# A fused decoder layer in float32: pads between the tiles of split weights, and a smaller tile of ones

## The chip, the cores and the metric

The kernel runs on one core of a Trainium2 chip. Five engines work side by side: TensorE (PE in the profile, its weight loads PEld), VectorE (DVE), ScalarE (ACT), GpSimd (POOL) and SyncE (SP), which here issues all DMA transfers. Tiles lie in the on-chip buffer, 128 partitions of some 224 KB each; every tile has one start address that is the same in all partitions, and where this text speaks of addresses it means that one, in bytes. Products are summed in PSUM. The metric is the time of one execution on the device in microseconds: the median of three runs. Matmuls are counted start to start where their pace is meant; the duration that the profile gives for one is longer, since they are pipelined.

## What is computed

One layer of a decoder trunk on a sequence of 1,024 positions and 1,024 features, all in float32:

```python
h = rmsnorm(x, mix_norm)
q, k, v, su, sv, g_a, g_b = split(h @ w_in)          # 512, 128, 128, 512, 512, 1024, 1024 columns
y_att = sliding_window_attention(q, k, v, ...)       # 8 query heads, 2 key heads, window 128
y_sgu = gelu(su) * (tril(w_s) @ rmsnorm(gelu(sv)) + b_s)
merged = sigmoid(g_a) * (y_att @ w_oa) + sigmoid(g_b) * (y_sgu @ w_ob)
x = x + merged @ w_out
z = conv3(rmsnorm(x) @ w_up)                          # 1024 -> 2 * 2816, causal width 3 per channel
x = x + (silu(z_gate) * z_val) @ w_down
```

## The kernel before

**Split products.** A float32 product is made of three matmuls in a format (R in the code) that keeps fewer bits: each operand is split into a rounded part h and a rest l, and h·h, h·l and l·h are summed. ACT copies the tile into h (`copy_hi`, line 75), POOL or DVE subtracts (for weights `wsplit`, line 91, and `Left.split`, line 975). So weights exist as a raw tile, an h tile and an l tile, 128 partitions by 1,024 numbers (4,096 bytes) each.

**Stages.** (1) k, v and q projections while x arrives (matmuls of 256 columns; `pkv`, `pq`), beside them the row sums of x squared, in `rstd_b`, a buffer of one row of 1,024 numbers that later holds the norm's factor. (2) Attention in blocks of 128 queries, with the u projection (`pu`) as filler. (3) The v projection of the spatial gate (`pvs`), whose second half of weights, `wvB`, lies in the pool zr on the right side of the buffer, and the mixing (`pm`). (4) The gates, from 221 us: each pair of column blocks is one step of a 2 by 2 Strassen-like scheme (`Blocks`, line 1000, its matmuls at line 1017) with seven products of twelve matmuls of 512 columns; the moving operands are B11, B21, B22 and the sums T1 to T4, of which T3 now lies in zr; the stationary ones are the split weights p (A11, A12), q (S1, A22), s3 (S3) and r (S2, S4; its halves lie in a tile AX). (5) Eight branch products twice and eight output tiles, `po` and `px` (lines 79 to 81), by a list of jobs. (6) 22 pairs of the up projection, with the same scheme as the gates (`fast_pair`, line 1489), T3 now in another pool (ex), s3 in a pool wx; the convolution and the gating run on DVE and ACT beside them. (7) The down projection (line 1661), again seven products.

**Order.** PE's order is written by hand from stage 2 on (`manual_schedule`), and the other engines' order too from there; in stage 1 a scheduler sets the order of the engines other than PE. SP's queue carries all DMAs in program order.

**Allocation.** A pool lays its tiles out in the order in which the program first asks for them, rounded up to 32 bytes. From the bottom stand: `base` (constants, `ones`, `rstd_b`, small columns, `msk`), `big` (eight tiles of 16,384 bytes: x, weights of q, later all large row tiles), `wst` (the split weights), then pools that are opened and closed by stage; from the top stand the right side's pools. In `wst` come three raw tiles, then, by tag and with two buffers each, h, h, l, l; a request with a tag takes the buffer that is free next. Tiles of 32 bytes named pad_l, pad_r and pad_z stand in three stage pools. Modulo 512, all of `big` and `wst` start at 0 (xf at 7,680, the raw tiles from 138,752, h at 151,040 and 155,136, l at 159,232 and 163,328); zr's tile starts at 212,928, which is 448 modulo 512.

**At the start.** POOL fills `ones` (128 by 128) and `mh05`; PE does seven warm-up products of `ones` with `ones` (line 209) while the first x is on its way; `affine_select` (line 150) makes the mask from `ones`; `ssq` (line 306) and `ssq_cols` (line 1343) use two columns of it.

Of the kernel before, what the change touches and what calls it, by code (L numbers as in the profile page):

```python
# [10 lines left out]
F = mybir.dt.float32  # L11
R = mybir.dt.float32r
# [22 lines left out]
def build(tc, a):  # L35
    nc = tc.nc
    ctx = ExitStack()
    with ctx, tc.manual_schedule(engines={mybir.EngineType.PE}):
        body(ctx, tc, nc, a)


def body(ctx, tc, nc, a):
    L, H = slice(0, 512), slice(512, 1024)
    base = ctx.enter_context(tc.tile_pool(name="base", bufs=1))
    big = ctx.enter_context(tc.tile_pool(name="big", bufs=1))
    wst = ctx.enter_context(tc.tile_pool(name="wst", bufs=2))
# [3 lines left out]
    def nm(s):  # L50
        uid[0] += 1
        return f"{s}_{uid[0]}"

    def Y(s, dt=R, shape=None):
        return big.tile(shape or [128, 4, 1024], dt, tag="Y", name=nm(s), bufs=7)
# [10 lines left out]
    def PH(s):  # L66
        if psum.get("H") is None:
            return PS(s)[:, 0:512]
        return psum["H"].tile([128, 512], F, tag="H", name=nm(s))

    def raw(s):
        return wst.tile([128, 8, 128], F, tag="raw", name=nm(s), bufs=3)

    def copy_hi(dst, src, scale=1.0):
        return nc.scalar.activation(dst, src, AF.Copy, scale=scale)  # L75

# [11 lines left out]
    def wtile(src, s, nk=8):  # L88
        return wsplit(wload(src, s, nk), s, nk)

    def wsplit(r, s, nk=8):

        h = wst.tile([128, 8, 128], R, tag="wh", name=nm(s + "h"))
        l = wst.tile([128, 8, 128], R, tag="wl", name=nm(s + "l"))
        copy_hi(h[:, :nk, :], r[:, :nk, :])
        nc.gpsimd.tensor_tensor(l[:, :nk, :], r[:, :nk, :], h[:, :nk, :].bitcast(F), op=ALU.subtract)  # L96
        return h, l
# [2 lines left out]
    cp = base.tile([128, 194], F, name="cp")  # L100
    sink_b = base.tile([128, 8], F, name="sink_b")
    ident = base.tile([128, 128], F, name="ident")
    ones = base.tile([128, 128], F, name="ones")
    rstd_b = base.tile([128, 1024], F, name="rstd_b")
    mh05 = base.tile([128, 8], F, name="mh05")
    rstd = base.tile([128, 8], F, name="rstd")
    nc.gpsimd.memset(ones, 1.0)
    nc.gpsimd.memset(mh05, -0.5)
    g2 = cp[:, 0:8]
# [3 lines left out]
    def rsqrt_cols(dst, ss, n, width):  # L113

        nc.vector.tensor_scalar(dst, ss, 1.0 / width, EPS, op0=ALU.mult, op1=ALU.add)
        return nc.gpsimd.tensor_tensor(dst, dst, mh05[:, :n], op=ALU.pow)
# [3 lines left out]
    def rms_rows(pb, col, hs=(0, 1)):  # L120
# [6 lines left out]
        for h, p in zip(hs, pb):  # L127
# [19 lines left out]
    kTl = kp.tile([128, 2, 1024], R, name="kTl")  # L147
    ali = kp.tile([128, 8, 128], F, name="ali")
    kp.tile([128, 8], F, name="pad_r")
    nc.gpsimd.affine_select(out=ali[:, 0:4, :], in_=ones.unsqueeze(1).to_broadcast([128, 4, 128]),  # L150
                            pattern=[[0, 4], [1, 128]], compare_op=ALU.is_gt, fill=0.0, base=0,
                            channel_multiplier=-1)
    nc.vector.tensor_copy(msk, ali[:, 0:4, :])
# [27 lines left out]
    sqsum = rstd_b  # L181
# [13 lines left out]
    def xsquare(k):  # L195
        for c in (L, H):
            xs = xr[k][:, 257 + c.start:257 + c.stop]
            if k == 0:
                nc.scalar.activation(sqsum[:, c], xs, AF.Square)
                continue  # L200
            sq = PH("sq")
            nc.scalar.activation(sq, xs, AF.Square)
            nc.vector.tensor_tensor(sqsum[:, c], sqsum[:, c], sq, op=ALU.add)
# [2 lines left out]
        xload(k)  # L206
    warm = PH("warm")
    for _ in range(7):
        nc.tensor.matmul(warm[:, 0:128], ones, ones, start=True, stop=True)
    xcuts = {0: (slice(0, 256), slice(256, 512), slice(512, 1024))}  # L210
    for k in range(8):
        x1 = xr[k]
# [26 lines left out]
        if k == 6:  # L239
            rsplit(wq[0], rwq[1], 1)  # L240
    xsquare(7)
    u_next = [wst.tile([128, 8, 128], R, tag="wh", name="u0h"), wst.tile([128, 8, 128], R, tag="wl", name="u0l")]
    copy_hi(u_next[0], u_raw[0])
    nc.vector.tensor_tensor(u_next[1], u_raw[0], u_next[0].bitcast(F), op=ALU.subtract)

# [57 lines left out]
    man.__enter__()  # L303
    p_ssq = PH("ssq")
    for s in range(8):
        nc.tensor.matmul(p_ssq[:, 2 * s:2 * s + 2], sqsum[:, s * 128:(s + 1) * 128], ones[:, 0:2],
                         start=True, stop=True)
    q_proj(0)
    q_proj(1)
# [265 lines left out]
    def weights(n):  # L575

        for i, x in enumerate(items):
            if WHEN.get(x) != n:
                continue
            if x == "q0":  # L580
                wq.append(Y("wq", R, [128, 2, 8, 256]))
            if x == "v0":
                wv.append(Y("wv", R, [128, 2, 8, 256]))
            if x == "z0":
                qp_cm.__exit__(None, None, None)
                kp_cm.__exit__(None, None, None)
                zr_cm.append(tc.tile_pool(name="zr", bufs=1, side="right"))
                zr.append(zr_cm[0].__enter__())
                wv.append(zr[0].tile([128, 2, 8, 256], R, tag="Z", name="wvB"))
                zr[0].tile([128, 8], F, name="pad_z")  # L590
            if x[0] == "u":
                ust[("w", int(x[1]))] = wsplit(raws[x], "wu")
            elif x[0] == "q":
                rsplit(wq[1], raws[x], int(x[1]))
            elif x[0] == "v":
                rsplit(wv[0], raws[x], int(x[1]))
            elif x[0] == "z":
                rsplit(wv[1], raws[x], int(x[1]))
            load_ahead(i + 3)
# [93 lines left out]
    def job_split(i):  # L693
        if i < len(jobs):
            nk = jobs[i][1]
            if nk:
                job_w[i] = wsplit(job_w[i], "wj", nk)
            else:
                for _ in job_w[i]:
                    pass  # L700
# [22 lines left out]
    vsh = sg.tile([128, 8, 512], R, name="vsh")  # L723
    vsl = sg.tile([128, 8, 512], R, name="vsl")
    wr = raws["s"]
    wgh = wst.tile([128, 8, 128], R, tag="wh", name="wgh")
    wgl = wst.tile([128, 8, 128], R, tag="wl", name="wgl")
    vg_, vss_ = {}, {}
    xb = {"B11": xq[0][0], "B21": xq[1][0], "B22": xq[1][1]}

# [154 lines left out]
    pools = {"dr": dr}  # L885
# [31 lines left out]
    class Left:  # L917
# [61 lines left out]
                self.w[n] = tuple(t[:, 4 * j:4 * j + 4] for t in (h, l))  # L979

        def split_p(self):
            self.split(("A11", "A12"), self.p, *(wst.tile([128, 8, 128], R, tag="w" + x, name=nm("p" + x))
                                                 for x in "hl"))

        def split_q(self):
            self.split(("S1", "A22"), self.q, *(wst.tile([128, 8, 128], R, tag="w" + x, name=nm("q" + x))
                                                for x in "hl"))

        def split_s3(self):
# [232 lines left out]
    def open_out():  # L1222
        pools["mg_cm"].__exit__(None, None, None)
        pools["ls_cm"].__exit__(None, None, None)
        s3_cm.__exit__(None, None, None)
        pools["wx"] = pools["hx"] = ctx.enter_context(tc.tile_pool(name="wx", bufs=1, reuse_waits="tile"))
        pools["ex"] = ctx.enter_context(tc.tile_pool(name="ex", bufs=1, reuse_waits="tile"))
        pools["fp_cm"] = tc.tile_pool(name="fp", bufs=1, reuse_waits="tile")
        fp = pools["fp"] = pools["fp_cm"].__enter__()
        for n in ("B11", "T1", "B21", "B22"):  # L1230
            comb[n] = Y(n, R, [128, 2, 4, 512])
        comb["T3"] = pools["ex"].tile([128, 2, 4, 512], R, tag="T3", name="T3")
        pools["raw2"], pools["raw4"] = (fp.tile([128, 4, 512], F, name=n) for n in ("T2f", "T4f"))
        pools["sq2"] = fp.tile([128, 1024], F, name="sq2")
        dr = pools["dr"]
        pools["x2"] = [dr.tile([128, 1024], F, tag=f"x2_{d}", name=f"x2_{d}") for d in range(8)]
        for n in ("B11", "B21", "B22", "T1", "T2", "T3", "T4"):
            pools["d" + n] = [dr.tile([128, 512], F, tag=f"{n}_{i}", name=f"{n}_{i}") for i in range(HK)]
        out_load(D_ORDER[0])
        psum["P"].insert(0, psum["P"].pop())  # L1240
# [6 lines left out]
    def out_load(d):  # L1247
        acs[d] = pools["fp"].tile([128, 1024], F, tag="ac", name=nm("ac"), bufs=2)
        nc.sync.dma_start(acs[d], a["xw"][d, :, 257:1281])
# [5 lines left out]
    def out_tile(i):  # L1255
        d = D_ORDER[i]

        def main(w):
            if i == 0:
                open_out()  # L1260
# [79 lines left out]

    def ssq_cols(p):
        for s in range(8):
            nc.tensor.matmul(p[:, 2 * s:2 * s + 2], pools["sq2"][:, s * 128:(s + 1) * 128], ones[:, 0:2],
                             start=True, stop=True)
        pool = pools["fp"]
        ss = pool.tile([128, 8], F, name="ss8b")
        nc.vector.tensor_copy(ss, p[:, 0:16].rearrange("p (s two) -> p s two", two=2)[:, :, 0])
        rsqrt_cols(ss, ss, 8, D)
        nc.vector.reciprocal(rstd, rstd)
        nc.vector.tensor_tensor(ss, ss, rstd, op=ALU.mult)  # L1350
        return ss
# [80 lines left out]
    def first_pair():  # L1432
# [35 lines left out]
        q.prod(q.v1, "S2", "T2", more=True)  # L1468
        pb = q2.zv
        ratio = ssq_cols(pb)  # L1470
        nx.sums_r()
        nx.split_q()
# [362 lines left out]
```

## Time and profile before

| | |
|---|---|
| median of 3 runs | 1194.94 us (1194.39 to 1196.06) |
| profiled execution | 1196.25 us |
| its span, first to last instruction | 1194.5 us |
| PE busy | 1182.8 us, 99% of the span, 5,890 matmuls |
| DVE, ACT, POOL busy | 881.3, 541.9, 567.0 us |
| granted PE clock | 1.0 of full speed |
| DMA engines' mean busy share | 46% |

A row of the groups reads: line, engine, operation, output tile <- input tiles (buffer numbers left out, so T is T1 to T4, x the tiles of the first input), shapes, how many, then busy time and mean duration of one in ns, then idle time before. A row of the timeline: start and duration in us, engine, line, operation, tiles, shape, count. A row of the windows: stretch, length, then busy time and instructions of PE, PEld, DVE, ACT and POOL, PE's granted clock, DMA share and GB/s. A row of the chain: start, duration, what. A row of the waits: who waited for whom, us in total, times, longest.

### The profile page before, as it was taken

The numbers are of one execution on the slowest core, as the hardware profiler recorded it, in microseconds if no ns is written. First come the engines' busy times: TensorE is split into PE (matmuls) and PEld (weight loads), VectorE is DVE, ScalarE is ACT, GpSimd is POOL, SyncE is SP. The second block draws the span as 40 slices with busy tenths as digits, with TensorE's granted clock in tenths as the row PEclk, the third lists the DMA queues.
The fourth block names the chain that finished last, engine by engine and source line by source line (L and its number), as shares of the span: only waits on it lengthen the run. The fifth ranks groups of instructions, "written<-read, shape, count | busy, mean of one in ns | idle before, by whom it ended". The sixth has DMA issues, their size and how long they took to land.

```text
span 1194.5 us, 15884 instructions
## 1 busy us (share of the span) xinstructions
PE 1182.8 (99%) x5890; PEld 1002.5 (84%) x5890; DVE 881.3 (74%) x1028; ACT 541.9 (45%) x832; POOL 567.0 (47%) x363
## 2 busy tenths in 40 slices
PE   8999999999999999999999999999999999999998
PEld 8989989988888888888888888888888888888886
DVE  7688975746648665668897788878788798775674
ACT  8555567644335222234544444444444545435331
POOL 2367685488768222344756575656657551000000
PEclk9999999999999999999999999999999999999999
DMA  7010133037686987342143242423333268965471
GB/s 272 34 54 19 54 131 135 4 129 252 244 318 209 356 315 283 128 160 104 54 141 109 103 140 99 149 89 123 108 130 124 88 215 289 368 229 194 152 232 66
DMA packets 79133, 191.27 MB, mean 160 GB/s; under 512 B 8912, under 2 KB 9168, under 8 KB 79056
## 3 DMA queue, kind: packets, MB, share of 16 engines
q1 hardware_dynamic: 79056, 190.26, 45.5%
q8 instruction: 46, 0.75, 0.3%
q14 instruction: 31, 0.25, 0.1%
HBM read 139.63 MB, written 50.59 MB: 159 GB/s over the span
## 4 chain that ended last, share of the span: by engine, by line
PE 90%; DVE 5%; ACT 2%; issue 1%; POOL 1%; DMA 1%; SPq 0%; POOLq 0%; ACTq 0%; DVEq 0%
PE pz L1017 48%; PE pd L1661 10%; PE pdy L1661 8%; PE px L81 2%; PE px L80 2%; PE po L81 2%; PE po L80 2%; PE po L79 2%; PE px L79 2%; PE pvs L79 1%; PE pvs L81 1%; PE pvs L80 1%; PE pq L79 1%; PE pq L81 1%; PE pq L80 1%
## 5 line engine op out<-in xcount | busy, mean ns | idle before, releaser
L1017 PE MATMUL pz<-T,qh 128*128 128x512 f32 x472 | 145.5, 390 | 0.0
L977 POOL TENSOR_TENSOR pl<-lp,ph 128x1024 fp32r<-128x1024 f32 x30 | 72.6, 2420 | 81.9 <-ACT ph L75 81.7
L1017 PE MATMUL pz<-B,ph 128*128 128x512 f32 x352 | 109.2, 391 | 0.0
L1017 PEld LDWEIGHTS pz<-T,qh 128*128 128x128 f32 x472 | 88.4, 188 | 18.6 <-ACT u L868 0.3
L1017 PE MATMUL pz<-T,ql 128*128 128x512 f32 x236 | 91.8, 389 | 0.0
L96 POOL TENSOR_TENSOR wjl<-wj,wjh 128x512 fp32r<-128x512 f32 (+1 forms) x24 | 40.4, 1682 | 96.2 <-ACT wjh L75 96.2
L977 POOL TENSOR_TENSOR ql<-lq,qh 128x1024 fp32r<-128x1024 f32 x30 | 77.0, 2568 | 9.1 <-ACT qh L75 9.1
L1017 PEld LDWEIGHTS pz<-B,ph 128*128 128x128 f32 x352 | 65.3, 188 | 15.1 <-ACT x L1508 2.0
L1033 DVE TENSOR_TENSOR pz<-pz,rstd_b 128x1024 f32<-128x1024 f32 x60 | 73.9, 1232 | 4.2 <-ACT rstd_b L128 2.1
L977 POOL TENSOR_TENSOR s3l<-s,s3h 128x512 fp32r<-128x512 f32 x29 | 38.9, 1342 | 71.2 <-ACT s3h L75 59.1
L1017 PE MATMUL pz<-T,s3h 128*128 128x512 f32 x232 | 71.7, 390 | 0.0
L1017 PE MATMUL pz<-B,pl 128*128 128x512 f32 x176 | 68.5, 389 | 0.0
L1661 PE MATMUL pd<-bh,ah 128*128 128x512 f32 x176 | 68.5, 389 | 0.0
L1661 PE MATMUL pd<-bl,ah 128*128 128x512 f32 x176 | 68.5, 389 | 0.0
L1661 PE MATMUL pd<-bh,al 128*128 128x512 f32 x176 | 68.5, 389 | 0.0
L1017 PE MATMUL pz<-T,AX 128*128 128x512 f32 x264 | 63.4, 389 | 0.0
L1017 PE MATMUL pz<-B,AX 128*128 128x512 f32 x264 | 63.4, 389 | 0.0
L1017 PEld LDWEIGHTS pz<-T,AX 128*128 128x128 f32 x264 | 49.5, 188 | 10.3
L1017 PEld LDWEIGHTS pz<-B,AX 128*128 128x128 f32 x264 | 49.5, 188 | 10.3
L1367 DVE SCALAR_TENSOR_TENSOR tg<-pz,cp,tg 128x1023 f32<-128x1023 f32 (+1 forms) x44 | 56.2, 1277 | 0.8
L1367 DVE SCALAR_TENSOR_TENSOR tv<-pz,cp,tv 128x1023 f32<-128x1023 f32 (+1 forms) x44 | 56.2, 1277 | 0.8
L977 POOL TENSOR_TENSOR AX<-lr,AX 128x1024 fp32r<-128x1024 f32 x22 | 53.7, 2441 | 5.1 <-ACT AX L75 5.1
(341 smaller groups left out, 3518.0 us busy)
## 6 DMA issues: line engine op xcount, KB each, us to landing
ls<-wup SPq DMA_DIRECT2D x22, 512.0 KB, 5.9
sum<-ls SPq DMA_DIRECT2D x22, 512.0 KB, 5.1
lp<-wup SPq DMA_DIRECT2D x22, 512.0 KB, 3.5
ra<-wdown SPq DMA_DIRECT2D x44, 256.0 KB, 4.6
b<-T SPq DMA_DIRECT2D x44, 256.0 KB, 3.9
B<-tv SPq DMA_DIRECT2D x33, 256.0 KB, 2.0
T<-tt SPq DMA_DIRECT2D x33, 256.0 KB, 2.0
b<-B SPq DMA_DIRECT2D x33, 256.0 KB, 3.6
```

Source lines behind the costliest of these rows:

```text
L79: nc.tensor.matmul(out, wh, mh, start=first, stop=False, **kw)
L80: nc.tensor.matmul(out, wh, ml, start=False, stop=False, **kw)
L81: nc.tensor.matmul(out, wl, mh, start=False, stop=last, **kw)
L96: nc.gpsimd.tensor_tensor(l[:, :nk, :], r[:, :nk, :], h[:, :nk, :].bitcast(F), op=ALU.subtract)
L977: nc.gpsimd.tensor_tensor(l, r, h.bitcast(F), op=ALU.subtract)
L1017: nc.tensor.matmul(o, p[:, k, :], y[:, q, k, :], start=not more and k == 0 and j == 0, stop=k == 3 and j == 2, skip_group_check=True)
L1033: nc.vector.tensor_tensor(z, z, rstd_b, op=ALU.mult)
L1367: nc.vector.scalar_tensor_tensor(t[:, j:], p[:, 0:1024 - j], cw[:, ci, 2 - j:3 - j], t[:, j:], op0=ALU.mult, op1=ALU.add)
L1661: nc.tensor.matmul(o[d], p[:, k - k0, m], q[:, k - k0, :], start=new and k == 0 and j == 0, stop=k == HK - 1 and j == 2, skip_group_check= ...
```

## The change

The split weights get one tag per buffer and stand in the order h0, l0, h1, l1, with a pad of 64 bytes ahead of each; a counter alternates between the two buffers. The pool wx gets a pad of 64 bytes ahead of each of s3h and s3l, and both stand ahead of its other tiles. `ones` keeps two columns and moves behind `rstd_b`; the warm-up products and the mask take their ones from the first 128 columns of `rstd_b`, which POOL fills at the start and which the sums of squares overwrite.

```diff
+    raw_first = wst.tile([128, 8, 128], F, tag="raw", name="raw_first", bufs=3)
+    for i, x in enumerate(("h0", "l0", "h1", "l1")):
+        wst.tile([128, 16], F, tag=f"pad{x}", name=f"pad{x}", bufs=1)
+        wst.tile([128, 8, 128], R, tag=f"w{x}", name=f"first{x}", bufs=1)
+    w_n = {"h": 0, "l": 0}
+
+    def wt(x, s):
+        w_n[x] += 1
+        return wst.tile([128, 8, 128], R, tag=f"w{x}{w_n[x] % 2}", name=nm(s + x), bufs=1)
...
-        h = wst.tile([128, 8, 128], R, tag="wh", name=nm(s + "h"))
-        l = wst.tile([128, 8, 128], R, tag="wl", name=nm(s + "l"))
+        h, l = wt("h", s), wt("l", s)
...
-    ones = base.tile([128, 128], F, name="ones")
     rstd_b = base.tile([128, 1024], F, name="rstd_b")
+    ones = base.tile([128, 2], F, name="ones")
...
+    nc.gpsimd.memset(rstd_b[:, 0:128], 1.0)
     nc.gpsimd.memset(ones, 1.0)
...
-    nc.gpsimd.affine_select(out=ali[:, 0:4, :], in_=ones.unsqueeze(1).to_broadcast([128, 4, 128]),
+    nc.gpsimd.affine_select(out=ali[:, 0:4, :], in_=rstd_b[:, 0:128].unsqueeze(1).to_broadcast([128, 4, 128]),
...
-        nc.tensor.matmul(warm[:, 0:128], ones, ones, start=True, stop=True)
+        nc.tensor.matmul(warm[:, 0:128], rstd_b[:, 0:128], rstd_b[:, 0:128], start=True, stop=True)
...
-        nc.tensor.matmul(p_ssq[:, 2 * s:2 * s + 2], sqsum[:, s * 128:(s + 1) * 128], ones[:, 0:2],
+        nc.tensor.matmul(p_ssq[:, 2 * s:2 * s + 2], sqsum[:, s * 128:(s + 1) * 128], ones,
...
-    wgh = wst.tile([128, 8, 128], R, tag="wh", name="wgh")
-    wgl = wst.tile([128, 8, 128], R, tag="wl", name="wgl")
+    wgh, wgl = wt("h", "wg"), wt("l", "wg")
...
-            self.split(("A11", "A12"), self.p, *(wst.tile([128, 8, 128], R, tag="w" + x, name=nm("p" + x))
+            self.split(("A11", "A12"), self.p, *(wt(x, "p")
...
         pools["wx"] = pools["hx"] = ctx.enter_context(tc.tile_pool(name="wx", bufs=1, reuse_waits="tile"))
+        for x in "hl":
+            pools["wx"].tile([128, 16], F, tag="pad" + x, name="pad" + x, bufs=1)
+            pools["wx"].tile([128, 4, 128], R, tag="s3" + x, name="first_s3" + x)
```

By these sizes the addresses become: xf at 7,200 and with it all of `big` at 32 modulo 512, the raw tiles too; h0 at 150,624, l0 at 154,784, h1 at 158,944, l1 at 163,104 (96, 160, 224 and 288 modulo 512); s3h and s3l of the pairs at 352 and 416, T3 of the pairs at 416; zr's tile stays at 448.

More of the change, by code (lines that the diff above doesn't have):

```diff
@@ L241, in body @@
     xsquare(7)
-    u_next = [wst.tile([128, 8, 128], R, tag="wh", name="u0h"), wst.tile([128, 8, 128], R, tag="wl", name="u0l")]
+    u_next = [wt("h", "u0"), wt("l", "u0")]
     copy_hi(u_next[0], u_raw[0])
@@ L981, in split_p @@
         def split_p(self):
-            self.split(("A11", "A12"), self.p, *(wst.tile([128, 8, 128], R, tag="w" + x, name=nm("p" + x))
+            self.split(("A11", "A12"), self.p, *(wt(x, "p")
                                                  for x in "hl"))
         def split_q(self):
-            self.split(("S1", "A22"), self.q, *(wst.tile([128, 8, 128], R, tag="w" + x, name=nm("q" + x))
+            self.split(("S1", "A22"), self.q, *(wt(x, "q")
                                                 for x in "hl"))
@@ L1342, in ssq_cols @@
         for s in range(8):
-            nc.tensor.matmul(p[:, 2 * s:2 * s + 2], pools["sq2"][:, s * 128:(s + 1) * 128], ones[:, 0:2],
+            nc.tensor.matmul(p[:, 2 * s:2 * s + 2], pools["sq2"][:, s * 128:(s + 1) * 128], ones,
                              start=True, stop=True)
```

## The prediction

> **What bounds the kernel now.** I read the page's busy times first, then the windows, the waits of PE, the chain, and last the starts of single matmuls in the timeline.
>
> ```profile
> span 1194.5 us, 15884 instructions
> PE 1182.8 (99%) x5890; PEld 1002.5 (84%) x5890; DVE 881.3 (74%) x1028; ACT 541.9 (45%) x832; POOL 567.0 (47%) x363
> ```
> ```profile
> 800.00:900.00 100.00, 100.00 (x442) 82.39 (x441) 83.92 (x80) 45.28 (x53) 62.56 (x32) 1.00 0.35 119
> ```
> ```profile
> PE pkv L79 <- ACT x L75: 1.5, 1, 1.5
> PE warm L209 <- POOL mh L108: 1.0, 1, 1.0
> ```
> ```profile
> 245.56 136.83 PE pz L1017 x600
> 581.89 397.92 PE pz L1017 x1752
> ```
>
> PE is busy 99% of the span, the longest wait it has is 1.5 us, and the chain runs through matmuls alone from 581.89 us on for 397.92 us. So PE's rate is the time: 1,752 matmuls of 512 columns in 397.92 us are 227.1 ns each, start to start. DVE has 26% of the span free, POOL 53%. No stall is there for this change to remove; only the spacing of the matmuls can move the total, and 1 ns on 4,403 of them is 4.4 us.
>
> Does spacing depend on where operands lie? The diff moves addresses and little else, so this is the question. All tiles' addresses follow from their sizes in order of allocation. Before, the row tiles (x, B11, T1, y, m, wdown's pieces) and the split weights (h, l, s3h, s3l, AX) all start at a multiple of 512 bytes. One pool is off: zr on the right side, whose tiles (wvB in the v phase, then T3 of the gates) start 64 bytes below a multiple of 512. Two pieces of the timeline, first T3 against its neighbours, then wvB against wkv (start, duration, line, tiles):
>
> ```profile
> 246.89 0.61 PE L1017 MATMUL pz<-T,qh 128*128 128x512 f32 x2
> ...
> 248.25 0.61 PE L1017 MATMUL pz<-x,ph 128*128 128x512 f32 x2
> ...
> 250.97 0.63 PE L1017 MATMUL pz<-T,s3h 128*128 128x512 f32 x2
> 251.44 0.39 PE L1017 MATMUL pz<-T,s3l 128*128 128x512 f32 x1
> ...
> 253.77 0.62 PE L1017 MATMUL pz<-x,ph 128*128 128x512 f32 x2
> ```
> ```profile
> 6.23 0.28 PE L79 MATMUL pkv<-wkv,x 128*128 128x256 f32 x1
> ...
> 6.95 0.28 PE L79 MATMUL pkv<-wkv,x 128*128 128x256 f32 x1
> ```
> ```profile
> 187.38 0.28 PE L79 MATMUL pvs<-wvB,x 128*128 128x256 f32 x1
> ...
> 188.74 0.28 PE L79 MATMUL pvs<-wvB,x 128*128 128x256 f32 x1
> ```
>
> From 246.89 to 248.25 lie six matmuls (T against qh, ql): 226.7 ns each. From 250.97 to 253.77 lie the twelve of S3 times T3: 233.3 ns each, 6.7 ns or 2.9% more, with no wait among them. The chain agrees: its stretch of gates from 245.56 holds seven such products (84 matmuls), which add 84 × 6.7 = 0.56 us, 0.93 ns on the mean of its 600; it has 228.05 ns against 227.1. With 256 columns the sign turns: wkv (level with its weights) takes 0.72 us for six, 120 ns each; wvB (64 below them) takes 1.36 us for twelve, 113.3 ns. So the trace shows that the distance of moving operand to weights decides a step of 6.7 ns per matmul, up at 512 columns and down at 256.
>
> The weights that are read while a matmul streams are the next one's:
>
> ```profile
> 6.00 0.28 PE L80 MATMUL pkv<-wkv,x 128*128 128x256 f32 x1
> 6.00 0.19 PEld L81 LDWEIGHTS pkv<-wkv,x 128*128 128x128 f32 x1
> ```
>
> The load for line 81's matmul starts with line 80's matmul. So what counts in a matmul's spacing is the distance of its moving tile to the next matmul's weights.
>
> **The change, part by part.**
>
> *Ones of two columns, memsets, warm-up on the row buffer.* POOL writes rstd_b's first 128 columns in the place of ones, then ones and mh.
>
> ```profile
> 0.79 0.20 POOL L107 MEMSET ones<- 128x128 f32 x1 [0.29 <-POOLq L1826]
> 0.93 0.10 POOL L108 MEMSET mh<- 128x8 f32 x1
> 1.05 3.35 PE L209 MATMUL warm<-ones 128*128 128x128 f32 x14 [1.05 <-POOL mh L108]
> ...
> 2.12 0.63 POOL L150 TENSOR_SCALAR_AFFINE_SELECT ali<-ones 128x512 f32<-128x512 f32 x1
> ```
> ```profile
> 5.48 0.62 ACT L199 ACTIVATE rstd_b<-xf 128x512 f32<-128x512 f32 x1
> 8.64 0.42 ACT L75 ACTIVATE wkv<-xf 128x256 fp32r<-128x256 f32 x1 [2.55 <-DMA xf<-xw]
> 10.19 0.61 ACT L199 ACTIVATE rstd_b<-xf 128x512 f32<-128x512 f32 x1
> ```
>
> One small memset more is 0.10 us on POOL; the warm-up waits for the first memset alone and ends at 4.4 us, POOL's mask at 2.75, and the second x tile arrives at 8.64. The square that overwrites those 128 columns now waits for the warm-up and the mask, both long done. In the built program that half square stands two ACT instructions later (behind wkv and the first x of k = 2), the other half stays in the idle time at 5.48. ACT's sum up to the third x is unchanged, so 0; ends -0.5 and +0.5 us (its own 0.52 us won or lost once). The order on PE and SP is otherwise the same, DVE swaps msk with one wkv.
>
> *Shift of the left pools.* The base pool shrinks by 480 bytes. Every left tile from xf on then starts at 32 modulo 64; moving and stationary tiles shift alike, so AX in the pairs and the whole down projection keep distance 0. No PE operand of the trace lies at 32 modulo 64, so no row prices this. The nearest rows say that only distances matter: I take 0. The other end is one more step of 6.7 ns for each 512-column matmul, 4,403 × 6.7 = 29.4 us (a row of 2,048 bytes then straddles one more 64-byte piece); nothing speaks for a gain.
>
> *Pads between the split weights.* h and l of the two slots now lie 64, 128, 192 and 256 bytes above the row tiles (modulo 512). Distances of moving tile to next weights become -64 or -192 where the next is an h (p in one slot, q in the other, jobs alternate), -128 or -256 where it is an l. In the pairs T3 lies 64 above s3h and level with s3l. Matmuls whose weights are an h or s3h:
>
> ```profile
> L1017 PE MATMUL pz<-T,qh 128*128 128x512 f32 x472 | 145.5, 390 | 0.0
> L1017 PE MATMUL pz<-B,ph 128*128 128x512 f32 x352 | 109.2, 391 | 0.0
> L1017 PE MATMUL pz<-T,s3h 128*128 128x512 f32 x232 | 71.7, 390 | 0.0
> L79 PE MATMUL px<-mh,wjh 128*128 128x512 f32 x128 | 49.8, 389 | 0.0
> L80 PE MATMUL px<-ml,wjh 128*128 128x512 f32 x128 | 49.8, 389 | 0.0
> L1017 PE MATMUL pz<-x,ph 128*128 128x512 f32 x128 | 39.5, 390 | 0.0
> L79 PE MATMUL po<-bh,wjh 128*128 128x512 f32 x64 | 24.9, 389 | 0.0
> L79 PE MATMUL pu<-x,wuh 128*128 128x512 f32 x48 | 19.4, 404 | 0.0
> ```
>
> With po's three like groups (bl, ah, al, 64 each) the split h are 472 + 352 + 128 + 128 + 128 + 4 × 64 = 1,464; s3h in the pairs is 232 - 56 of the gates = 176. The u chunks are left out: they come in short bursts between waits and are off the even pace already (404 ns where the others have 389). The row for -64 is T3's: +6.7 ns. For -192 and +64 no row has 512 columns; they are odd multiples of 64 as -64 is, and I give them T3's price. For -128 and -256 I take 0, the price of distance 0, which they share as even multiples. Sum: (1,464 + 176) × 6.67 = **+10.9 us**. Lower end: -64 alone is dear, that is ph (352 + 128) and half of the jobs' 512, 736 × 6.67 = +4.9 us. Upper end: every shifted distance is dear, l too (half as many), 1.5 × 1,640 × 6.67 = +16.4 us; the gates' AX, now at -256, stays at 0. A gain as at 256 columns is the first rival.
>
> *The 256-column stages.* wvB is at -96 instead of -64 (192 matmuls) and the mixing weights wg at -64 instead of 0 (64): by the rows 113.3 and 120 between 0 and +1.3, and -0.4 us; I take 0.
>
> *DVE, ACT, POOL, DMAs.* Same instructions at other addresses, and all have idle time: the longest POOL split is covered by PE.
>
> ```profile
> L977 POOL TENSOR_TENSOR ql<-lq,qh 128x1024 fp32r<-128x1024 f32 x30 | 77.0, 2568 | 9.1 <-ACT qh L75 9.1
> ```
>
> If each took 10% longer, 0.26 us would go into POOL's free half; a pair is 84 matmuls, 19 us, with four splits. A DVE wait in the out projection stands one instruction earlier; 0.
>
> **Sum.** The profiled execution took 1196.25 us (span 1194.5); with +10.9 it would be 1207.1. It lies 1.3 us above the median of 1194.94, so the median becomes 1205.9.
>
> **The rivals.**
>
> *Faster: distance 0 is the conflict.* For it: wvB, 6.7 ns better than wkv. If at 512 columns -128 to -256 behave as -64 does at 256, all 1.5 × 1,640 = 2,460 matmuls win 6.67 ns: -16.4 us, 1178.5. It decides as soon as the mean over these falls 1 ns below 226.7. Against it: the only 512-column row off level is dearer, and -64 itself is among the new distances.
>
> *Slower by more: half pieces.* The 32-byte shift adds its step: 29.4 us on top, 1235 with the pads' part, and about 1214 to 1226 if it costs half of that. For it: the step of 6.7 ns is some 16 columns' worth (226.7 / 512 × 16 = 7.1 ns), and 16 columns of 4 bytes are 64 bytes. Against: no row.
>
> *No change.* Addresses do not matter to PE: 1195. The Trainium skill says so ("SBUF — State Buffer", Who interferes with whom: PE and ACT never wait on anyone; "TensorE: Matmul & The Clock Gate", Step-by-step, gives the weight load a read port of its own). By that rule the pads are worth 0 us; by T3's row they are worth 10.9. This trace disagrees with the rule, 233.3 against 226.7 ns with no wait between, so I leave it little.
>
> **Chances.** Forecast (+4.9 to +16.4) 0.53, half pieces 0.17, faster 0.24, no change 0.06. A change of 0.2% (2.4 us) is about what a measurement of this kernel can tell. Slower 0.70, same 0.06, faster 0.24. Without the faster case my range would be 1199 to 1232; to hold 8 in 10 it takes in most of the faster one, 1182 to 1230.
>
> **What would show it.** Right: ph against x or B spaced at 233 ns, as T3 was; about 435 matmuls per 100 us in the pairs instead of 442 (40 of a pair's 84 matmuls dearer by 6.7 ns); the last 180 us (down projection, distance 0) as long as before. Wrong: the down projection slower too (half pieces), or spacings of 220 ns with ph and qh (the faster rival), or 226.7 everywhere. A new wait of PE would be a cause that I have not named.

## The result and the profile after

The changed kernel takes 1206.88 us (median of four executions, 1205.54 to 1207.03); the kernel before took 1194.66 us beside it (four executions, 1194.25 to 1196.06). The ratio is 1.0098 with a 95% interval of 1.0080 to 1.0115: slower by 1%, where 1205.9 us was forecast. The profiled execution took 1206.9 us.

The page of the kernel after: its span, and the busy times of the engines.

```profile
span 1205.2 us, 15888 instructions
PE 1193.6 (99%) x5890; PEld 1005.1 (83%) x5890; DVE 878.8 (73%) x1028; ACT 543.9 (45%) x832; POOL 566.7 (47%) x364
```

PE has the same 5,890 matmuls and is busy 10.8 us longer (1193.6 against 1182.8); the span has grown by 10.7. DVE and POOL are as busy as before within 3 us, and POOL has one instruction more. The waits of PE, the longest two:

```profile
PE pkv L89 <- ACT x L85: 1.8, 1, 1.8
PE warm L219 <- POOL mh L118: 1.0, 1, 1.0
```

There is no new wait of PE. The warm-up waits 1.0 us as before, and the first k, v product 0.3 us longer. So the time went into the matmuls themselves. The chain of the kernel after (start, length, engine, line, number of matmuls) and one row of the chain before:

```profile
246.47 138.35 PE pz L1026 x600
...
587.77 403.09 PE pz L1026 x1752
...
1140.63 57.81 PE pd L1673 x255
```
```profile
1130.16 57.81 PE pd L1661 x255
```

The 1,752 matmuls of the pairs take 403.09 us, 230.1 ns each, where they took 227.1. The 600 of the gates take 1.52 us more. The end of the down projection, which uses none of the padded tiles, takes 57.81 us both times. One window inside the pairs says the same in matmuls per 100 us: 436 where there were 442.

```profile
800.00:900.00 100.00, 100.00 (x436) 81.71 (x435) 83.30 (x80) 45.94 (x54) 59.41 (x30) 1.00 0.35 118
```

From the start of each stage's first matmul to that of the next, in the two traces:

| stage | before, us | after, us | difference |
|---|---|---|---|
| k and v of the attention | 27.84 | 28.17 | +0.33 |
| attention, u projection | 151.78 | 151.78 | 0.00 |
| v projection of the spatial gate | 37.77 | 38.36 | +0.59 |
| gates | 160.50 | 161.97 | +1.47 |
| branch products (jobs) | 87.04 | 88.70 | +1.66 |
| out projection | 87.04 | 88.51 | +1.47 |
| pairs | 423.33 | 428.85 | +5.51 |
| down projection | 214.90 | 214.48 | -0.42 |

The first stage, which waits for data, lasts between 26.5 and 28.2 us in all the traces of this study; differences of a single execution below 1.5 us in all are read by stage for that reason.

Below, a distance is the address of the moving tile minus that of the weights, and a spacing is the time from the start of one matmul to the start of the next, sorted by the distance of its moving tile to the next matmul's weights, as the prediction did. With 512 columns the trace after gives:

| distance in bytes | matmuls | mean spacing, ns | over the 226.9 of level tiles before, times the count, us |
|---|---|---|---|
| 0 | 1,550 | 227.4 | 0.8 |
| -64 | 762 | 232.4 | 4.2 |
| -128 | 401 | 229.4 | 1.0 |
| -192 | 810 | 230.4 | 2.8 |
| -256 | 589 | 229.9 | 1.8 |
| +64 (T3 on s3h) | 154 | 231.3 | 0.7 |

The sum is 11.3 us. It includes the u chunks of the attention, which cost that stage nothing; the four stages from the gates to the pairs grew by 10.1. T3 of the gates is not in the table: by the addresses it now lies 96 bytes below its weights instead of 64, and its 96 matmuls take what they took (233.6 ns on the mean, 233.4 before). These are not steps of one size, and the pace is no longer even. Part of the timeline of the kernel after, in the gates (start, duration, line, tiles; one row can hold two matmuls):

```profile
249.88 0.63 PE L1026 MATMUL pz<-x,ph 128*128 128x512 f32 x2
...
251.96 0.63 PE L1026 MATMUL pz<-T,s3h 128*128 128x512 f32 x2
...
254.76 0.62 PE L1026 MATMUL pz<-x,ph 128*128 128x512 f32 x2
```

From 249.88 to 251.96 lie nine matmuls of x with p, 231.1 ns each, where before they had 226.7. From 251.96 to 254.76 lie the twelve of S3 times T3, 233.3 ns each, exactly as before.

### The profile page after: what moved, and what is told of

Read it like the earlier page. It is cut to its first block, busy times and chain, and to the rows that moved or that the text cites. A ratio compares the mean times of both kernels' runs of the same rounds, so it can differ in the third digit from the quotient of the medians.

```text
span 1205.2 us, 15888 instructions
## 1 busy us (share of the span) xinstructions
PE 1193.6 (99%) x5890; PEld 1005.1 (83%) x5890; DVE 878.8 (73%) x1028; ACT 543.9 (45%) x832; POOL 566.7 (47%) x364
## 4 chain that ended last, share of the span: by engine, by line
PE 91%; DVE 5%; ACT 2%; issue 1%; DMA 1%; POOL 0%; SPq 0%; DVEq 0%; POOLq 0%; ACTq 0%
PE pz L1026 48%; PE pd L1673 10%; PE pdy L1673 7%; PE po L89 2%; PE px L89 2%; PE po L91 2%; PE px L91 2%; PE po L90 2%; PE px L90 2%; PE pvs L89 1%; PE pvs L91 1%; PE pvs L90 1%; PE pq L89 1%; PE pq L91 1%; PE pq L90 1%; ACT x L85 1%
## 5 line engine op out<-in xcount | busy, mean ns | idle before, releaser
L85 ACT ACTIVATE qh<-lq 128x1024 fp32r<-128x1024 f32 x30 | 31.8, 1061 | 80.9 <-POOL pl L986 49.3
L1026 PEld LDWEIGHTS pz<-T,AX 128*128 128x128 f32 x264 | 49.6, 188 | 10.8
```

What stands on the lines that cost most here:

```text
L1026: nc.tensor.matmul(o, p[:, k, :], y[:, q, k, :], start=not more and k == 0 and j == 0, stop=k == 3 and j == 2, skip_group_check=True)
```

## The experiments

**Without the pads.** The question is whether the smaller tile of ones, the memset, the warm-up on the row buffer and the shift of the left pools by 32 bytes cost anything by themselves. The kernel before gets the change without its pads:

```diff
-    ones = base.tile([128, 128], F, name="ones")
     rstd_b = base.tile([128, 1024], F, name="rstd_b")
+    ones = base.tile([128, 2], F, name="ones")
...
+    nc.gpsimd.memset(rstd_b[:, 0:128], 1.0)
...
-        nc.tensor.matmul(warm[:, 0:128], ones, ones, start=True, stop=True)
+        nc.tensor.matmul(warm[:, 0:128], rstd_b[:, 0:128], rstd_b[:, 0:128], start=True, stop=True)
...
```

> The kernel before with the small tile of ones, the memset and the warm-up on the row buffer, and no pads: all left tiles start at 32 modulo 64, their distances to each other stay 0; only the tiles of zr change their distance to x, from -64 to -96. Theory 'distance alone counts': the even pace of 226.7 ns stays in gates, jobs, pairs and down projection; the v phase loses some 0.6 us (the changed kernel had it 0.59 us longer); 1195 to 1196 us. Rival 'half pieces', that a start at 32 modulo 64 costs by itself: 6.7 ns for each 512-column matmul outside the down projection, 1200 us or more.

Measured: 1196.05 us (ten executions) against 1195.2, ratio 1.0009 (0.9999 to 1.0018). Its chain:

```profile
244.97 136.87 PE pz L1018 x600
...
1129.43 57.81 PE pd L1662 x255
```

The gates take 136.87 us where before they took 136.83, the pairs 423.37 against 423.33. With every left tile at 32 modulo 64, level matmuls of 512 columns keep 227.0 ns on the mean. So the shift is free as such, the half pieces are ruled out, and the prologue costs nothing that can be measured. Only the v projection is longer, by 0.62 us: wvB now lies 96 bytes below its weights and takes 117.6 ns instead of 113.9.

**One distance for each slot.** Next the pads are regrouped: h and l of one slot lie side by side, at one distance from the row tiles, and the other slot at another; s3 has no pads. First 128 and 256 bytes.

```diff
-    for i, x in enumerate(("h0", "l0", "h1", "l1")):
-        wst.tile([128, 16], F, tag=f"pad{x}", name=f"pad{x}", bufs=1)
-        wst.tile([128, 8, 128], R, tag=f"w{x}", name=f"first{x}", bufs=1)
+    for i, gap in enumerate((128, 128)):
+        if gap:
+            wst.tile([128, gap // 4], F, tag=f"pad{i}", name=f"pad{i}", bufs=1)
+        for x in "hl":
+            wst.tile([128, 8, 128], R, tag=f"w{x}{i}", name=f"first{x}{i}", bufs=1)
...
```

> The changed kernel with other pads: h and l of one slot both 128 bytes above the row tiles, of the other slot both 256, no pads at s3h and s3l (T3 level with them). Theory of the prediction 'odd multiples of 64 are dear, even ones free': p, q, wj all at 226.7 ns, total as before, 1195 to 1196 us. Rival 'only level is even': p, q and wj lose the even pace and take 229 to 231 ns on the mean (the changed kernel had 229.4 where the next weights lay at 128 and 229.9 at 256), some 2,300 matmuls by 2.7 to 3.2 ns, +6 to +8 us, 1201 to 1203 us. If the pattern repeats after 256 bytes, q alone (256) keeps 226.7.

Measured: 1203.44 us (one execution). The pairs' row of its chain:

```profile
585.68 401.77 PE pz L1028 x1752
```

They are 3.85 us longer than before. Sorted by distance, the 1,162 matmuls against tiles at 128 bytes are spaced 232.7 ns, the 1,404 against tiles at 256 bytes 227.9, most of these 226 or 227. So an even multiple of 64 bytes is not free: 128 is nearly as dear as T3's 64 (233.4 ns), and 256 is nearly level.

**64 and 192.** The same with `(64, 128)` for the two gaps.

> As the one before with 64 and 192 bytes. Theory of the prediction: h and l alike at 233.3 ns, 2,300 matmuls by 6.7 ns, +15 us, 1210 us. Rival 'only level is even': the means that the changed kernel showed, 232.4 ns at 64 and 230.4 at 192, so +5.7 and +3.7 ns, about +11 us, 1206 us, the spacings scattered and not one value.

Measured: 1206.19 us (one execution). Spacings: 233.4 ns at 64 and 229.3 at 192. A piece of its timeline in the gates, first q (192 above), then p (64 above):

```profile
246.49 0.62 PE L1028 MATMUL pz<-T,qh 128*128 128x512 f32 x2
...
247.86 0.63 PE L1028 MATMUL pz<-x,ph 128*128 128x512 f32 x2
...
250.66 0.63 PE L1028 MATMUL pz<-T,s3h 128*128 128x512 f32 x2
```

Six matmuls with q take 1.37 us, 228.3 ns each; twelve with p take 2.80 us, 233.3 each. So 64 bytes cost what T3's row said when h and l both lie there, and 192 cost a third of it, though both are odd multiples.

**320 and 384.** The same with `(320, 64)`, to see whether the pattern repeats after 256 bytes.

> As before with 320 and 384 bytes. Theory of the prediction: 320 (odd) at 233.3 ns, 384 (even) at 226.7, 1202 us. Rival 'only level is even': both scattered at 229 to 232 ns, 1202 to 1205 us. If some distance is better than level (a gain as wvB had at 256 columns) it shows as a spacing under 226 ns.

Measured: 1209.95 us (one execution); 233.2 ns at 320 and 232.2 at 384, against 233.4 at 64 and 232.7 at 128. Its timeline in the gates, p at 320:

```profile
248.31 0.63 PE L1028 MATMUL pz<-x,ph 128*128 128x512 f32 x2
...
251.11 0.62 PE L1028 MATMUL pz<-T,s3h 128*128 128x512 f32 x2
```

The twelve matmuls with p take 2.80 us again, 233.3 ns each. It repeats. This is the slowest kernel of the study, as both slots lie at a dear distance; its pairs are 6.65 us longer than before.

**256 for all.** One pad of 256 bytes ahead of all four tiles, none between them.

```diff
-    for i, x in enumerate(("h0", "l0", "h1", "l1")):
-        wst.tile([128, 16], F, tag=f"pad{x}", name=f"pad{x}", bufs=1)
-        wst.tile([128, 8, 128], R, tag=f"w{x}", name=f"first{x}", bufs=1)
+    wst.tile([128, 64], F, tag="pad", name="pad", bufs=1)
+    for i in range(2):
+        for x in "hl":
+            wst.tile([128, 8, 128], R, tag=f"w{x}{i}", name=f"first{x}{i}", bufs=1)
...
```

> The changed kernel with one pad of 256 bytes ahead of all four split-weight tiles in the place of the four pads of 64, none at s3h and s3l. Theory 'the pattern repeats after 256 bytes': p, q and wj keep the even pace of 226.7 ns, jobs and out projection as long as before (87.0 us each), total as with the small ones alone, 1195 to 1197 us. Rival 'level alone is even, q at 256 kept its pace by its place among its neighbours': p and wj at 229 to 232 ns, 1201 us or more.

Measured: 1196.16 us (ten executions) against 1195.6, ratio 1.0002 (0.9993 to 1.0012). Its chain:

```profile
245.21 136.85 PE pz L1027 x600
...
581.55 397.94 PE pz L1027 x1752
```

Gates and pairs are as before to 0.02 us, with 2,566 matmuls at 256 bytes spaced 227.1 ns. What counts is the distance modulo 256 bytes, and of the multiples of 64 only 0 keeps the even pace.

**Without the s3 pads.** The changed kernel, less the two pads in the pool wx.

```diff
-        for x in "hl":
-            pools["wx"].tile([128, 16], F, tag="pad" + x, name="pad" + x, bufs=1)
-            pools["wx"].tile([128, 4, 128], R, tag="s3" + x, name="first_s3" + x)
```

> The changed kernel without the pads at s3h and s3l of the pairs (T3 level with both again), the pads of the split weights as changed. If each tile's distance has its own price: 176 matmuls with s3h next get back the 4.6 ns that they lost (231.3 ns in the changed kernel), 0.8 us, the pairs 4.7 us longer than before instead of 5.5, total 1206.1. If the uneven pace carries over from the products around: the pairs stay 5.5 us longer, 1206.9.

Measured: 1204.99 us (one execution). Its chain:

```profile
246.00 138.35 PE pz L1026 x600
...
587.19 401.78 PE pz L1026 x1752
```

The gates are as after (138.35), the pairs' row 1.31 us shorter than after (their stage 1.42). That is what T3 off the level of s3h cost, near the 1.2 us of the forecast (176 times 6.67 ns). In the changed kernel it is spread otherwise: the 176 matmuls with s3h take 5.4 ns more than before, the 88 with s3l, for which nothing was forecast, 4.0 more.

**l alone off level.** h of both slots level with the row tiles, l of both 128 bytes above, no s3 pads.

```diff
...
+    for x in "hl":
+        for i in range(2):
+            wst.tile([128, 8, 128], R, tag=f"w{x}{i}", name=f"first{x}{i}", bufs=1)
+        if x == "h":
+            wst.tile([128, 32], F, tag="pad", name="pad", bufs=1)
...
```

> The changed kernel with the h tiles level with the row tiles and the l tiles 128 bytes above, no pads at s3h and s3l. Of the three matmuls of a step (h by hi, h by lo, l by hi) only the second has an l as its next weights, only the third has it as its own. 'The next weights count': the second is the slow one, near 232.7 ns, and first and third are nearer to 227. 'The own weights count': the third is. The prediction's theory (128 is free): 226.7 throughout, 1196 us. Total else 1200 to 1203 us.

Measured: 1207.71 us (one execution), above the expectation: as dear as the whole change (its four stages from the gates to the pairs lose 11.3 us), though only a third of the matmuls of these products have an l as weights. The timeline shows where, for a product of B and p:

```profile
701.68 0.62 PE L1028 MATMUL pz<-B,ph 128*128 128x512 f32 x2
702.14 0.40 PE L1028 MATMUL pz<-B,pl 128*128 128x512 f32 x1
702.38 0.62 PE L1028 MATMUL pz<-B,ph 128*128 128x512 f32 x2
```

The two matmuls with h take 0.46 us, the one with l 0.24: 0.70 in all where three at the even pace take 0.68. Sorted by both neighbours over the whole trace: 2,502 matmuls level with their own weights and with the next ones are spaced 227.3 ns; 801 level with their own but 128 off the next 232.4; 754 that are 128 off their own but level with the next 234.0. So the prediction's rule, that the next weights decide, is half of it. A matmul loses its pace beside weights off level on either side, and each lone l costs two spacings.

**The same, l's together.** If so, fewer changes between h and l must cost less, at the same addresses. Each product of the gates and pairs now sends its eight matmuls with h first, then its four with l; the jobs stay as they were.

```diff
-            for k in range(4):
-                for j, (p, q) in enumerate(((wh, 0), (wh, 1), (wl, 0))):
+            for n, (k, p, q) in enumerate([(k, wh, q) for k in range(4) for q in range(2)] +
+                                          [(k, wl, 0) for k in range(4)]):
...
```

> The kernel with h level and l 128 bytes up, but each product of twelve matmuls sends its eight with h first and its four with l after them; the jobs keep their order. If a matmul is slow wherever its own weights or the next ones are off level, five of twelve are slow instead of eight: about +3.3 us in the pairs (instead of +5.3), +1.6 us in the gates (instead of +2.6), 1204.5 to 1205 us in all. If only the next weights count, or only its own, it is four of twelve in both orders, and the time stays within 0.7 us of the 1207.7 of the plain order.

Measured: 1204.69 us (one execution). Its chain, and then that of the plain order:

```profile
245.24 138.62 PE pz L1028 x600
...
586.97 401.61 PE pz L1028 x1752
```
```profile
246.28 139.21 PE pz L1028 x600
...
588.68 402.96 PE pz L1028 x1752
```

The two rows are 0.59 and 1.35 us shorter; jobs and out projection, whose order was left, take 88.75 us each in both kernels. The order by itself costs nothing where all is level: the products with AX in the pairs keep 226.7 to 227.0 ns. The count of spacings with weights off level on either side (own or next) fell from 1,735 to 1,375, and neither one-sided rule gives a gain.

The stages kept more of their loss than five eighths (five slow spacings of twelve instead of eight): +1.9 instead of +1.6 us in the gates, +3.9 instead of +3.3 in the pairs. The two traces show where that lies. In the gates the pad of 128 bytes also moves gax, the tile that holds the weights S2 and S4; its 180 matmuls, 180 of the counted spacings in either kernel, cost 1.0 us over those of the kernel before in the plain order and 0.9 in the new one. In the pairs the products of S3 and T3 are level themselves, but they follow products that are not, and cost 1.2 us more than before in both kernels. Without these parts the loss falls from 1.6 to 1.0 us in the gates and from 4.1 to 2.7 in the pairs, and five eighths would be 1.0 and 2.6. (Of the 3.0 us between the two times, another 1.3 lie in the first stage, 26.6 us against 27.9.)

**T3 level.** The kernel before with a row of 192 bytes more in zr, so that T3 lies 256 bytes below its weights, modulo 512 (as good as level, by the kernel with 256 for all), and wvB stays where it was.

```diff
-                wv.append(zr[0].tile([128, 2, 8, 256], R, tag="Z", name="wvB"))
+                z = zr[0].tile([128, 4144], R, tag="Z", name="wvB")
+                wv.append(z[:, 48:4144].rearrange("p (j k c) -> p j k c", j=2, c=256))
...
```

> The kernel before with a tile of the pool zr that is 192 bytes longer: wvB stays 64 bytes below a multiple of 256, T3 of the gates becomes level with the weights. If distance makes T3's 233.3 ns: its 96 matmuls fall to 226.7, 0.64 us, and the uneven matmuls behind each product go too, 7 times some 20 ns; the gates 0.7 to 0.8 us shorter than before, total 1194.3 against 1195.1 (0.07%, at the edge of what 5 rounds tell). If T3 is slow for another reason (its pool, its place): the gates unchanged at 160.5 us.

Measured: 1194.97 us (eleven executions) against 1195.6, ratio 0.9993 (0.9984 to 1.0002). T3 takes 227.0 ns instead of 233.4, and the gates' row in the chain is 0.34 us shorter than before:

```profile
245.07 136.49 PE pz L1021 x600
```

The stage gained 0.43 us, less than expected: 96 × 6.4 ns are 0.61. In this execution one of the 96 spacings is 312 ns, which takes some 0.09 back; the rest stayed open. In the total it can't be told from nothing.

**The v projection.** The changed kernel with 224 bytes more in the base pool: wvB is 64 bytes below its weights again, and no left tile is at 32 modulo 64.

```diff
+    base.tile([128, 56], F, name="pad_b")
```

> The changed kernel with 224 bytes more in the base pool, so that every left tile is at a multiple of 256 bytes again and the zr tiles at 64 below, as before the change; the pads stay. If the v phase's +0.6 us comes from wvB at 96 below its weights instead of 64, that stage takes 37.8 us instead of 38.4 and the kernel about 1206.3 us; the gates, the jobs, the out projection and the pairs keep their +1.5, +1.7, +1.5 and +5.5 us. If the odd 32 bytes and the pads act together on the even pace, the 512-column stages come back as well, below 1203 us.

Measured: 1204.91 us (one execution). The v stage takes 37.77 us, as before the change; gates +1.33, jobs +1.66, out +1.47, pairs +5.51, as with the change. The timelines at wvB, one matmul of three, of the changed kernel and then of this one:

```profile
186.08 0.28 PE L89 MATMUL pvs<-wvB,x 128*128 128x256 f32 x1
...
189.60 0.28 PE L89 MATMUL pvs<-wvB,x 128*128 128x256 f32 x1
```
```profile
186.19 0.28 PE L89 MATMUL pvs<-wvB,x 128*128 128x256 f32 x1
...
188.23 0.28 PE L89 MATMUL pvs<-wvB,x 128*128 128x256 f32 x1
```

In the first, thirty matmuls take 3.52 us, 117.3 ns each; in the second, eighteen take 2.04 us, 113.3 each. The v stage's +0.6 us is wvB's move from 64 to 96 bytes, and the odd 32 bytes have no part in the pads' cost.

**Using it.** If 256 columns run faster at 64 bytes below the weights, wq (both halves) and wv can be put there too. The kernel before, with T3 level, the small ones for the room, and an offset in the tiles that hold wq and wv:

```diff
...
+        n = SLOT[uid[0]]
+        o = {"Y0": 0 if s == "wq" else 16, "Y2": 48 if s in ("wq", "wv") else 0}.get(n, 0)
+        y = big.tile([128, {"Y0": 4112, "Y2": 4160}.get(n, 4096)], dt, tag=n, name=name, bufs=1)
+        y = y[:, o:o + math.prod(shape[1:])]
...
```

(`SLOT` names, for each row tile, the buffer that it had before.)

> The kernel before with only the 256-column moving tiles wq, wq of the second half and wv put 64 bytes below the level of their weights (as wvB is), ones of two columns for the room, T3 level. If the distance sets the spacing in the same way wherever 256 columns are used, 561 matmuls go from 119.6 to about 114 ns: 3.1 us less in the attention and v stages, with 0.4 us less in the gates about 1191.5 us, ratio 0.997. If the 113.3 ns are special to wvB (its stage, or its pool on the right), or if these stages wait on other engines, it stays within 1 us of the time before.

Measured: 1194.11 us (eleven executions) against 1195.57, ratio 0.9990 (0.9981 to 0.9999). It is the only kernel here whose interval lies below the one before, by 0.1%, and much less than expected. Two pieces of its timeline, one matmul of three in each:

```profile
169.00 0.28 PE L91 MATMUL pvs<-wv,x 128*128 128x256 f32 x1
...
171.03 0.28 PE L91 MATMUL pvs<-wv,x 128*128 128x256 f32 x1
```
```profile
188.40 0.28 PE L91 MATMUL pvs<-wv,x 128*128 128x256 f32 x1
...
189.81 0.28 PE L91 MATMUL pvs<-wv,x 128*128 128x256 f32 x1
```

The same tile at the same distance takes 112.8 ns in the first piece (eighteen in 2.03 us) and 117.5 in the second (twelve in 1.41 us). Over the trace wq and wv have 116.8 ns instead of 119.5, and wvB fell back from 113.9 to 117.3. The attention gained 0.68 us, the gates 0.67, the v stage lost 0.36. Distance alone does not set the pace of 256 columns; which of the two paces a product falls into is left open.

## Why the prediction was right, and where it was not

*PE's rate is the time; no new wait.* Right. PE's busy time and the span grew by the same amount (10.8 and 10.7 us), and the list of waits is the old one. The cover named for DVE and POOL held.

*Ones, memset, warm-up: 0.* Right: the kernel without pads is within 0.2% of before, and what it loses is in the v stage.

*Shift by 32 bytes: 0; half pieces as a rival.* Right; that rival is ruled out twice, by the kernel without pads and by the down projection (57.81 us for its last 255 matmuls in every kernel quoted).

*The 256-column stages: 0, with 0 to +1.3 for wvB.* It was +0.6, inside the bounds, and by the mechanism named.

*The pads: +10.9.* The total is right, +10.1 us in the four stages that they touch, and the s3 pads are right by themselves (1.2 forecast, 1.3 to 1.4 measured). But the step below it, "odd multiples of 64 at T3's price, even multiples at that of distance 0", is wrong in form. The runs put this in its place: only distance 0 modulo 256 keeps the pace, 128 costs as much as 64 (232.7 and 233.4 ns when a slot lies there whole), 192 less (229.3), and the weights on both sides of a matmul count, not the next ones alone. In the changed kernel h and l lie at different distances from the same row tile, and the values mix: the matmuls whose next weights are an h cost about 7.0 us (4.2 + 2.8) where 9.8 were forecast, those whose next are an l 2.8 us where none were. The two misses offset each other, so that the total came out so near is luck. The near hit on the s3 pads is of the same kind, as s3l took a share. The forecast's sign of it, "ph against x or B at 233 ns", came out as 231.8 on the mean of the 479 matmuls with ph; "40 of a pair's 84 dearer by 6.7" as a loss spread over all of them, 0.25 us per pair (5.51 / 22) where 0.27 was meant.

*The upper end, l as dear as h (+16.4),* was nearest to the kernel with 320 and 384, whose four stages lose 14.2 us; 1.0 of it lies in gax, which that bound left at 0.

*The rival "faster: distance 0 is the conflict".* It fell: no distance off level with more than 25 matmuls of 512 columns had a mean spacing below that of level tiles in the same kernel. At 256 columns its observation is true and worth little (0.1%).

*No change.* The rule that was quoted there (the Trainium skill, "SBUF — State Buffer", Who interferes with whom: PE waits for no other engine) would, read as the prediction reads it, give the same time wherever the pads lie. 1196.16 us with 256 bytes and 1203.44 with 128 and 256 disagree with that reading; with the rule's own words they don't, as the waits of PE are the old ones.

*The median.* The medians differ by 12.2 us, the profiled executions by 10.65; the execution of before that was profiled was 1.6 us above its median, that of after at its own. The first stage, which moves by as much between executions, would account for this, but that was not traced.

## What to carry to other kernels

Where PE is busy throughout, look at the start-to-start spacing of matmuls, not at their durations or waits: 3 ns on some 4,000 of them were 1% here and appeared in no list of waits. For matmuls of 512 columns in this format, keep moving tiles and both halves of the split weights at the same address modulo 256 bytes; a pad is free at 256 bytes and dear at 64, 128 or 192. A pad also moves every tile that is laid out behind it, as it did with gax. A price taken from one row holds for that distance and that order of matmuls: a single run with one distance for a whole slot would have shown that the rule of odd and even does not hold.

## What the runs showed of the hardware

The spacing of 512-column matmuls in this format depends on the distance of moving tile and weights modulo 256 bytes: 226.9 to 227.4 ns on the mean at 0 and 256 where the neighbours lie there too, 233.2 to 233.4 with the weights 64 or 320 above, 232.2 to 232.7 at 128 and 384, 229.3 at 192, with no new wait in the profile. T3 of the gates adds odd multiples of 32: 233.7 ns at 96 bytes below its weights (the kernel without pads), 233.1 at 32 above (the one with 320 and 384). It is not the distance of h to l that costs: with 64 and 192 both of a slot lie level with each other and are slow all the same. The trace doesn't show by what mechanism.

The even paces are steps of one size: 113.3, 120.0, 226.7 and 233.3 ns are 17, 18, 34 and 35 times 6.67 ns. Off level the pace is mostly uneven, with single spacings mostly between 225 and 241 ns, and the means above are means over such a mix. After an interruption, or behind an off-level product, a level sequence also needs some matmuls to get back: with l alone off level, a product of S3 and T3 in the pairs has spacings of 238, 233, 236, 224, 231, 236, 228, 233 and 231 ns before 226 and 227 follow.

At 256 columns and 64 bytes below, two paces, 112.8 and 117.5 ns, were seen for one moving tile at one distance; what decides between them stays open.
